# Hybrid attention block: the key and value projections as one unit of 512 columns, and the norm and rotation of the keys moved into the delta rule

## The chip, the cores and the metric

The kernel runs on one core of one Trainium2 chip. The metric is the device time of one execution in microseconds (us), as a median of several runs. The engines are TensorE (PE, with its weight loads as PEld), VectorE (DVE), ScalarE (ACT), GpSimd (POOL), and SyncE (SP), on whose queue all DMAs are issued. Each engine works through its instructions in order.

## What is computed

One layer of a decoder on x of 1024 tokens by 1024 channels, all in float32:

```python
h = rms_norm(x, norm_mix_g)
proj = h @ w_in
...
a_q = apply_partial_rope(rms_norm(a_q.reshape(B, S, ATT_HEADS, ATT_HEAD_DIM), q_norm_g), cos, sin)
a_k = apply_partial_rope(rms_norm(a_k.reshape(B, S, ATT_KV_HEADS, ATT_HEAD_DIM), k_norm_g), cos, sin)
a_v = a_v.reshape(B, S, ATT_KV_HEADS, ATT_HEAD_DIM)
...
o_att = dsa_sparse_attention(a_q, a_k, a_v, i_q, i_k, i_w)
merged = jax.nn.sigmoid(gate_a) * o_gdn + jax.nn.sigmoid(gate_b) * o_att
x = x + merged @ w_out
h2 = rms_norm(x, norm_mlp_g)
x = x + jnp.square(jax.nn.relu(h2 @ w_mlp_up)) @ w_mlp_down
```

proj is split into twelve parts, a_q (1024 columns), a_k (256) and a_v (256) among them. o_gdn is a gated delta rule over 8 heads (convolution, chunks of 64 tokens, a triangular solve, a scan of the state). The sparse attention scores every key for each query with a small indexer (i_q, i_k, i_w), takes the 256 best keys and attends to these alone.

## The kernel before

**Precision.** Each float32 operand of a projection is split into a high and a low part (hi, lo), and a product is three matmuls: hi by hi, hi by lo, lo by hi. ACT makes the high part of a weight (w<-wraw or w<-w), DVE the low part as the difference. The normed, transposed input stays in SBUF as ht_hi and ht_lo (hh and hl in the profile).

**Order of the work.** First the norm and transposition of x. Then the projections of the indexer and of the attention, in units: misc (unit 0), iq0 and iq1 (units 1 and 2, the indexer's queries), aq0 and aq1 (units 3 and 4, 512 columns each, called WIDE), ak (unit 5) and av (unit 6), 256 columns each. Beside them run the indexer's scores (sq<-ikh,iqt on PE, irl on ACT, sc on DVE) and the search for the 256th best score (tkcm passes on ACT, tkeq passes on DVE). Then come the eight heads of the delta rule, for which 48 units of 48 matmuls (gdense, dd<-hh,w) are put between as filler, then the attention, the output projection and the MLP.

**A unit.** The 1024 tokens are 8 blocks of 128, in two halves. For each block, dense and wide_dense add 8 tiles of 128 channels by three matmuls each, 24 matmuls, in one PSUM bank (name dd, two buffers), and ACT drains the bank to SBUF (drain, into tiles named pj and iq). A block of the units ak and av is 256 columns wide, so two blocks share a bank. In a WIDE unit the weights come in four pairs p of channel tiles; wide_weights casts the pair p of the next unit once the event ("pd", u - 1, p) says that the last matmul that uses it is issued. The ak and av weights are loaded and cast by weights, in two halves.

**After a unit.** proj_post takes four blocks of queries (or all eight of the keys): squares with row sums on ACT (hj), an inverse root in small steps on DVE (hss, hr, hrt), the product with it on DVE (pj<-pj,hr), the product with the gain on POOL (pj<-pj,qng, for the keys pj<-pj,kng), the rotation on POOL (ras, pj<-pj,ropeA), and a store to DRAM (QD, KD). The values (av) are stored as they come (VD).

**What sets the order.** All instructions are issued through Weave, a list scheduler that runs when the kernel is built: chains of work with priorities wait for events, each instruction has a modelled duration, and the result is one fixed order for each engine. It models no wait for a PSUM bank; such waits come from the tile framework, which makes a writer of a tile wait for the tile's earlier readers, whatever part of it they touch. The projections have priority 9, so they fill what the other chains leave. As all instructions pass one helper, they have one line in the profile (L2399), and are told apart by the names of their tiles.

**The end of the projections.** gweights loads and splits the weights of gdense; its first two units wait for the last projections' weights to be used, since they take the same slots. The scheduler runs until ak and av are stored, the tiles of this phase are given back, and the delta rule's chains are added. keys(h) is one of them; for every third head its tile um lies in slot 3.

Of the kernel before, what the change touches and what calls it, by code (L numbers as in the profile page):

```python
# [50 lines left out]
def body(tc, a, out, dbg=None):  # L51
# [51 lines left out]
    def rsq_w(pl, dst, src, n, tag, apart=True):  # L103
        t = pl.tile([P, max(n, 4)], F32, name=tag + "t")[:, :n]
        V_.tensor_scalar(dst.bitcast(I32), src.bitcast(I32), -0.5, float(0x5F3759DF), op0=OP.mult, op1=OP.add)
        for _ in range(3):
# [6 lines left out]
            if apart:  # L113
# [5 lines left out]
             + [("aq0", [(0, C_AQ, HALF)]), ("aq1", [(0, C_AQ + HALF, HALF)]), ("ak", [(0, C_AK, 256)]), ("av", [(0, C_AV, 256)])])  # L119
    WIDE = range(3, 5)  # L120
# [25 lines left out]
    kng = ix.tile([P, P], F32, name="kng")  # L146
# [18 lines left out]
    def loads():  # L165
# [31 lines left out]
        SY_.dma_start(kng, a["k_norm_g"].to_broadcast([P, P]))  # L197
# [131 lines left out]
    def weights(us):  # L329
        for u in us:  # L330
            yield
            if u == 5:
                yield ("pw", 4, 3)
            if u > 1:
                if u != 5:
                    yield ("pdense", u - 2)
# [11 lines left out]
            for js in ((0, 1),) if u == 1 else [(j,) for j in range(KT // kn)]:  # L348
                if u == 5:
                    yield ("pd", 4, js[0])  # L350
                yield "A"
                for j in js:
                    A_.activation(sp[j][0], sp[j][2], AF.Copy)
                if u == 1:
                    wv.done("w1hi")
                yield
                for j in js:
                    hi, lo, src = sp[j]
                    eng, nm = (G_, "G") if 0 else (V_, "V")
                    if u != 1:  # L360
                        yield nm
                    eng.tensor_tensor(lo, src, hi.bitcast(F32), op=OP.subtract)
                    hk += [hi[:, k, :] for k in range(kn)]
                    lk += [lo[:, k, :] for k in range(kn)]
                    if u in (1, 5):
# [3 lines left out]
            if u in (1, 5):  # L369
                load(u + 1)  # L370
# [10 lines left out]
    def wide_weights():  # L381
# [9 lines left out]
        for u in WIDE:  # L391
            for p in range(4):
# [11 lines left out]
                if u + 1 in WIDE:  # L404
                    wide_load(u + 1, p)
                elif p == 1:
                    load(u + 1)

    def wide_dense():
        for u in WIDE:  # L410
            for tb in range(NB):
                half, o = tb // 4, (tb % 4) * P
                if o == 0:
                    if u == 4:
                        yield ("stored", 3, 0) if half else ("score", 0)
                    outs[u, half] = ix.tile([P, 4, HALF], F32, name="iq" if u == 4 and half == 0 else "pj", bufs=2)
                    wv.add(3, proj_post(("pout", u, 4 * half + 3), (u, half), "aq", outs[u, half], 4 * half, 4, 4))
                ps = pd.tile([P, HALF], F32, name="dd")
                n = 0
                for k in range(KT):  # L420
                    if tb == 0 and k % 2 == 0:
                        yield ("pw", u, k // 2)
                    hi, lo = (t[:, k % 2, :] for t in whl[u, k // 2])
                    h_, l_ = ht_hi[k][half][:, o:o + P], ht_lo[k][half][:, o:o + P]
                    for l, r in ((h_, hi), (h_, lo), (l_, hi)):
                        PE_.matmul(ps, l, r, start=n == 0, stop=n == 3 * KT - 1)
                        n += 1
                        yield 0.0
                    if tb == NB - 1 and k % 2:
                        wv.done("pd", u, k // 2)  # L430
                wv.add(1, drain(outs[u, half][:, tb % 4, :], ps, ("pout", u, tb)))
            wv.done("pdense", u)

    def dense():
        jobs = [(0, 0), (1, 0), (0, 1), (1, 1), (1, 2)]
        jobs += [(2, t) for t in range(3)] + [(3, 0)] + [(u, t) for u in (5, 6) for t in range(4)]
        for u, t2 in jobs:
# [3 lines left out]
            nm = units[u][0]  # L441
# [11 lines left out]
            yield ("pwj", u, 0) if u in (1, 5) and t2 == 0 else ("pw", u)  # L453
# [15 lines left out]
            if t2 == 0:  # L469
                if nm[0] == "i":  # L470
                    outs[u] = ix.tile([P, 6, 256], F32, name="iq", bufs=2)
                    wv.add(1, iq_post(u - 1, outs[u]))
                else:
                    yield ("stored", 3, 1) if u == 5 else ("score", 1)
                    outs[u] = ix.tile([P, NB, 256], F32, name="pj" if u == 5 else "iq", bufs=2)
                    wv.add(3, proj_post(("pout", u, 3), (u,), nm, outs[u], 0, NB, 2))
# [3 lines left out]
            for j, ks in ((0, (0, 4)), (1, (0, 4)), (0, (4, KT)), (1, (4, KT))) if one else ((0, (0, KT)), (1, (0, KT))):  # L480
                tb = (2 if nm[0] == "i" else 0) + 2 * t2 + j
                half, o = tb // 4, (tb % 4) * P
                n = 3 * ks[0]
                for k in range(*ks):
                    if u == 1:
                        yield ("ht", half, k)
                        yield ("pwj", u, k // 4)
                    if u == 5 and t2 == 0:
                        yield ("pwj", u, k // 4)
# [188 lines left out]
    def proj_post(ready, key, nm, t, b0, nb, nh):  # L678
        yield ready
        dst = {"ak": KD, "av": VD, "aq": QD}[nm].rearrange("(b p) c -> p b c", p=P)[:, b0:b0 + nb, :]  # L680
        if nm == "aq":
            c0 = (key[0] - 3) * HALF
            dst = dst[:, :, c0:c0 + HALF]
        if nm != "av":
            gain = kng if nm == "ak" else qng
            v = t.rearrange("p b (h d) -> p b h d", h=nh)
            g = t.rearrange("p b (h d) -> p (b h) d", h=nh)
            ss = ix.tile([P, nb, nh], F32, name="hss", bufs=2)
            for b in range(nb):
                yield "A"  # L690
                for hh in range(nh):
                    junk = ix.tile([P, P], BF16, name="hj")
                    A_.activation(junk, v[:, b, hh, :], AF.Square, accum_out=ss[:, b, hh:hh + 1])
            yield
            sf = ss.rearrange("p b h -> p (b h)")
            V_.tensor_scalar(sf, sf, 1.0 / P, EPS, op0=OP.mult, op1=OP.add)
            yield
            r = ix.tile([P, nb, nh], F32, name="hr", bufs=2)
            rf = r.rearrange("p b h -> p (b h)")
            yield from rsq_w(ix, rf, sf, 16, "hr")  # L700
            yield
            V_.tensor_tensor(g, g, rf[:, :, None].to_broadcast([P, 16, P]), op=OP.mult)
            yield
            G_.tensor_tensor(g, g, gain[:, None, :].to_broadcast([P, 16, P]), op=OP.mult)
            yield from rope(ix, v, ropeA, nb, b0, nh, 16, "ra", G_)
# [4 lines left out]
        wv.done("stored", *key)  # L710

# [122 lines left out]
    wv.add(1, weights(range(5, len(units))))  # L834
# [157 lines left out]
    def keys(h):  # L992
# [3 lines left out]
        if h > 1:  # L996
            yield ("join", h - 2)
        es = gp.tile([P, NB, P], F32, name="es", bufs=3)
# [324 lines left out]
    for u in (6, 5):  # L1323
        wv.run(until=("put", u))
# [1040 lines left out]

class Ring:
# [102 lines left out]
```

## Time and profile before

| what | value |
|---|---|
| median of 3 runs | 1791.11 us (1791.09 to 1791.8) |
| span of the profiled execution | 1790.2 us |
| PE busy | 1775.3 us, 99% |
| DVE, ACT, POOL busy | 72%, 57%, 31% |
| granted TensorE clock | 1.00 in all stretches shown |

The profile has one execution, for which the page gives the span alone; it is 0.9 us below the median of the runs. A row of a timeline gives the start, the length, the engine, the tile written and the tiles read, the shape, how many such instructions in a row, and in brackets the idle time before it with what ended it. Since a matmul's end overlaps the next one's start, the rate is read from start to start.

### The profile page before, as it was taken

To read this page: it belongs to the slowest core of one execution; us is meant where nothing else is said; L and a number is where in the kernel's file an instruction comes from. 1 tells how busy PE (TensorE), PEld (TensorE's weight loads), DVE (VectorE), ACT (ScalarE), POOL (GpSimd) and SP (SyncE) were. 2 spreads that over 40 slices of the span, in tenths; PEclk is the share of its full clock that TensorE was granted. 3 is DMA by queue.
4 is the path that set the end of the run, shared out by engine and by line. 5 is a ranking of instruction groups with operands and counts; after the bars stand their busy time and mean duration, and the time that the engine had idled before them with its cause. 6 is when DMAs were issued, how large, how long until landed. Compare 5 with 4: busy or idle time off the path is not lost. (4 is left out here: it accounts for less than half of the span.)

```text
span 1790.2 us, 27615 instructions
## 1 busy us (share of the span) xinstructions
PE 1775.3 (99%) x9841; PEld 1486.8 (83%) x9841; DVE 1285.6 (72%) x2758; ACT 1013.4 (57%) x2074; POOL 548.6 (31%) x772
## 2 busy tenths in 40 slices
PE   9999999999999999999999999999999999999999
PEld 7987898888888888888887888888888888888887
DVE  6547668867787887975368776887666668969673
ACT  7555757666666554453447666686666664333331
POOL 0005430843462424554013211232333222222230
PEclk9999999999999999999999999999999999999999
DMA  5201242232222222332356231225444459373241
GB/s 165 83 13 48 72 122 73 50 99 66 69 75 72 54 66 56 89 85 54 101 179 205 71 102 54 94 94 183 153 161 145 143 192 372 122 249 127 95 139 49
DMA packets 196412, 198.73 MB, mean 111 GB/s; under 512 B 45146, under 2 KB 140595, under 8 KB 196275
## 3 DMA queue, kind: packets, MB, share of 16 engines
q1 hardware_dynamic: 196258, 196.98, 35.1%
q8 instruction: 77, 1.26, 0.3%
q14 instruction: 61, 0.49, 0.1%
q10 hardware_dynamic: 16, 0.00, 0.0%
HBM read 141.17 MB, written 55.77 MB: 110 GB/s over the span
## 5 line engine op out<-in xcount | busy, mean ns | idle before, releaser
L2399 PE MATMUL dd<-hh,w 128*128 128x512 f32 x1552 | 513.1, 402 | 0.0
L2399 PEld LDWEIGHTS dd<-hh,w 128*128 128x128 f32 x1552 | 285.6, 189 | 52.7 <-issue 2.1
L2399 PE MATMUL dd<-hl,w 128*128 128x512 f32 x776 | 312.3, 402 | 0.0
L2399 ACT ACTIVATE m<-m 128x512 fp32r<-128x512 f32 (+1 forms) x240 | 139.8, 625 | 79.4 <-PE o L2399 29.8
L2399 PE MATMUL dd<-hh,m 128*128 128x512 f32 x520 | 173.3, 397 | 0.1
L2399 DVE TENSOR_TENSOR m<-m,m 128x512 fp32r<-128x512 f32 (+2 forms) x184 | 141.0, 793 | 38.9 <-ACT m L2399 33.6
L2399 PEld LDWEIGHTS dd<-hl,w 128*128 128x128 f32 x776 | 146.4, 189 | 25.5 <-issue 0.4
L2399 PE MATMUL dd<-w,hh 128*128 128x256 f32 (+1 forms) x704 | 165.1, 324 | 0.0
L2399 PEld LDWEIGHTS dd<-w,hh 128*128 128x128 f32 x704 | 118.1, 190 | 9.7 <-issue 0.5
L2399 POOL TENSOR_TENSOR sx<-sx,stmp 128x60 f32<-128x60 f32 (+24 forms) x248 | 118.4, 477 | 19.4
L2399 POOL TENSOR_TENSOR stmp<-sx,um 128x60 f32<-128x60 f32 (+24 forms) x186 | 87.5, 470 | 91.7 <-DMA um<-ZA 78.1
L2399 PE MATMUL dd<-w,hl 128*128 128x256 f32 (+1 forms) x352 | 114.3, 325 | 0.0
L2399 PEld LDWEIGHTS dd<-hh,m 128*128 128x128 f32 x520 | 96.6, 188 | 18.4 <-DVE w L2399 0.7
L2399 DVE TENSOR_SCALAR_CACHE_REDUCE tkeq<-sc,cand 128x384 f16<-128x384 f32 (+3 forms) x128 | 103.3, 807 | 1.2
L2399 PE MATMUL dd<-hl,m 128*128 128x512 f32 x260 | 102.6, 395 | 0.9 <-POOL hl L2399 0.9
L2399 POOL TENSOR_TENSOR m<-m,m 128x512 f32<-128x512 f32 x48 | 69.7, 1459 | 105.7 <-DVE m L2399 59.0
L2399 ACT ACTIVATE hh<-m 128x1024 fp32r<-128x1024 f32 x44 | 45.2, 1056 | 90.9 <-PE s L2399 42.0
L2399 ACT ACTIVATE ha<-m 128x1024 fp32r<-128x1024 f32 x44 | 45.3, 1056 | 86.0 <-PE o L2399 35.1
L2399 DVE TENSOR_TENSOR w<-w,w 128x1024 fp32r<-128x1024 f32 (+1 forms) x63 | 69.3, 1102 | 24.6 <-ACT w L2399 23.1
L2399 ACT ACTIVATE tkcm<-sc,cand 128x1024 f16<-128x1024 f32 (+1 forms) x64 | 69.8, 1091 | 24.2 <-DVE cand L2399 23.4
L2399 PE MATMUL o<-hh,m 128*128 128x512 f32 x248 | 79.7, 389 | 0.0
L2399 PEld LDWEIGHTS dd<-w,hl 128*128 128x128 f32 x352 | 67.0, 190 | 4.6
(433 smaller groups left out, 4381.5 us busy)
## 6 DMA issues: line engine op xcount, KB each, us to landing
HD<-m SPq DMA_DIRECT2D x112, 256.0 KB
m<-HD SPq DMA_DIRECT2D x56, 512.0 KB
w<-in_w_in_dram SPq DMA_DIRECT2D x48, 512.0 KB
m<-in_w_mlp_up_dram SPq DMA_DIRECT2D x33, 512.0 KB
m<-in_w_mlp_down_dram SPq DMA_DIRECT2D x16, 512.0 KB
w<-in_x_dram SPq DMA_DIRECT2D x10, 512.0 KB
wraw<-in_w_in_dram SPq DMA_DIRECT2D x4, 1024.0 KB
es<-GC SPq DMA_DIRECT2D x8, 512.0 KB
```

Source lines behind the costliest of these rows:

```text
L2399: ins = f(*args, **kw)
```

## The change

The units ak and av become one WIDE unit akv (unit 5) of 512 columns. Keys and values are stored raw by put_raw, half by half. The blocks 6 and 7 of every query unit are now computed in turn, six matmuls of one weight pair for one block and then for the other, and the four blocks of akv's second half likewise, in four banks that are the halves of two tiles named sq; ("pd", u, p) is given after the pair's last use there. The keys' norm, gain and rotation become keys_normed, a chain of priority 7 which starts with the delta rule: four chunks of two blocks, each loaded from KD, treated by the same steps (normed, the middle of the old proj_post) and stored back. Its tiles are carved out of slot 3 (Carve), so keys(2) waits for it. gweights waits for single weight pairs of akv. The core of the diff:

```diff
@@ -116,8 +116,8 @@
-             + [("aq0", [(0, C_AQ, HALF)]), ("aq1", [(0, C_AQ + HALF, HALF)]), ("ak", [(0, C_AK, 256)]), ("av", [(0, C_AV, 256)])])
-    WIDE = range(3, 5)
+             + [("aq0", [(0, C_AQ, HALF)]), ("aq1", [(0, C_AQ + HALF, HALF)]), ("akv", [(0, C_AK, HALF)])])
+    WIDE = range(3, 6)
...
     def wide_dense():
         for u in WIDE:
-            for tb in range(NB):
-                half, o = tb // 4, (tb % 4) * P
...
-                ps = pd.tile([P, HALF], F32, name="dd")
...
-                    for l, r in ((h_, hi), (h_, lo), (l_, hi)):
-                        PE_.matmul(ps, l, r, start=n == 0, stop=n == 3 * KT - 1)
...
-                wv.add(1, drain(outs[u, half][:, tb % 4, :], ps, ("pout", u, tb)))
+            for half in range(2):
+                if u > 3:
+                    yield (("score", 0), ("stored", 3, 0), ("stored", 3, 1), ("score", 1))[2 * (u - 4) + half]
+                outs[u, half] = ix.tile([P, 4, HALF], F32, name="iq" if (u, half) in ((4, 0), (5, 1)) else "pj", bufs=2)
+                wv.add(3, (proj_post if u < 5 else put_raw)(("pout", u, 4 * half + 3), (u, half), "aq", outs[u, half], 4 * half, 4, 4))
+                if u == 5 and half:
+                    bank = [t[:, c, :] for t in (ps_.tile([P, 2, HALF], F32, name="sq") for _ in range(2)) for c in range(2)]
+                    order = [(range(4), (p, p + 1)) for p in range(4)]
+                else:
+                    bank = {}
+                    order = [((i,), (0, 4)) for i in range(4 - 2 * half)] + [((2, 3), (p, p + 1)) for p in range(4) if half]
+                for tbs, ks in order:
+                    for i in tbs:
+                        if ks[0] == 0 and not (u == 5 and half):
+                            bank[i] = pd.tile([P, HALF], F32, name="dd")
...
+                            for k in (2 * p, 2 * p + 1):
...
+                                for n, (l, r) in enumerate(((h_, hi), (h_, lo), (l_, hi))):
+                                    PE_.matmul(bank[i], l, r, start=k == n == 0, stop=k == KT - 1 and n == 2)
...
+                            if half and i == 3:
+                                wv.done("pd", u, p)
+                        if ks[1] == 4:
+                            wv.add(1, drain(outs[u, half][:, i, :], bank[i], ("pout", u, 4 * half + i)))
             wv.done("pdense", u)
+
+    def put_raw(ready, key, nm, t, b0, nb, nh):
+        for i in range(nb):
+            yield ("pout", 5, b0 + i)
+        for dst, o in ((KD, 0), (VD, 256)):
+            SY_.dma_start(dst.rearrange("(b p) c -> p b c", p=P)[:, b0:b0 + nb, :], t[:, :, o:o + 256])
+        wv.done("put", *key)
...
+    def keys_normed():
+        for b0 in range(0, NB, 2):
+            pl = Carve(slot(3, [P, D], F32))
+            t, table, gain = (pl.tile(d, F32) for d in ([P, 2, 256], [P, 2, 2, 32], [P, P]))
+            kd = KD.rearrange("(b p) c -> p b c", p=P)[:, b0:b0 + 2, :]
+            SY_.dma_start(t, kd)
+            SY_.dma_start(table, a["c_ropea"][:, :, b0:b0 + 2, :])
+            SY_.dma_start(gain, a["k_norm_g"].to_broadcast([P, P]))
+            yield
+            yield from normed(pl, t, 2, 2, 0, table, gain)
+            yield
+            SY_.dma_start(kd, t)
+            yield
+        wv.done("knorm")
...
     def gweights():
-        yield ("pdense", len(units) - 2)
+        for p in range(2):
+            yield ("pd", len(units) - 1, p)
         gload(0)
         for u in range(len(gunits)):
             yield
             if u == 1:
-                yield ("pdense", len(units) - 1)
+                yield ("pd", len(units) - 1, 2)
...
         if h > 1:
             yield ("join", h - 2)
+        if h == 2:
+            yield ("knorm",)
...
-    for u in (6, 5):
-        wv.run(until=("put", u))
+    wv.run(until=("put", 5, 1))
+    wv.add(7, keys_normed())
```

PE in the second half of unit 3 (aq0). dd_1450 before is the bank of block 6; after, dd_1448 is that of block 6 and dd_1459 that of block 7. Before:

```order
L2399 MATMUL dd_1450<-w6_750,hh1_99 128x512
L2399 MATMUL dd_1450<-w2_749,hl1_100 128x512
L2399 MATMUL dd_1450<-w3_793,hh2_101 128x512
L2399 MATMUL dd_1450<-w7_794,hh2_101 128x512
L2399 MATMUL dd_1450<-w3_793,hl2_102 128x512
```

After:

```order
L2435 MATMUL dd_1448<-w2_747,hh1_99 128x512
L2435 MATMUL dd_1448<-w6_748,hh1_99 128x512
L2435 MATMUL dd_1448<-w2_747,hl1_100 128x512
L2435 MATMUL dd_1459<-w2_747,hh0_97 128x512 [waits Activation_49]
L2435 MATMUL dd_1459<-w6_748,hh0_97 128x512
L2435 MATMUL dd_1459<-w2_747,hl0_98 128x512
```

Block 7, which stood 24 matmuls behind block 6's first, starts after six, and its first matmul waits for ACT (the drain of block 5, which used that bank).

ACT at the same place: irl is the indexer's relu, pj<-dd the drain, iqs and iqt belong to the next indexer block, w to the weights of unit 4. Before:

```order
L2399 ACTIVATE irl<-sq 128x512 [waits DVE_49,PE_49] x4
L2399 ACTIVATE pj<-dd 128x512
L2399 ACTIVATE iqs<-iq 128x8x64
L2399 ACTIVATE iqt<-tp 128x512 [waits PE_49]
L2399 ACTIVATE pj<-dd 128x512 [waits PE_49]
```

After:

```order
L2435 ACTIVATE irl<-sq 128x512 [waits DVE_49,PE_49] x4
L2435 ACTIVATE pj<-dd 128x512
L2435 ACTIVATE w_1469<-wraw 128x1024 [waits DMAHW3_49,PE_49]
L2435 ACTIVATE iqs<-iq 128x8x64
L2435 ACTIVATE w_1489<-wraw 128x1024 [waits DMAHW4_49,PE_49]
L2435 ACTIVATE iqt<-tp 128x512 [waits PE_49]
```

Two casts of unit 4's weights have moved ahead of the transposed indexer tile (iqt), one of them ahead of iqs; the drain still stands behind four irl.

PE at the end of akv. sq_2307 holds blocks 4 and 5, and the rows are the last matmul of block 4's last six and the first five of block 5's. After:

```order
L2435 MATMUL sq_2307<-w1_2119,hl7_112 128x512
L2435 MATMUL sq_2307<-w1_2119,hh6_109 128x512
L2435 MATMUL sq_2307<-w5_2120,hh6_109 128x512
L2435 MATMUL sq_2307<-w1_2119,hl6_110 128x512 [waits Activation_49]
L2435 MATMUL sq_2307<-w1_2119,hh7_111 128x512
L2435 MATMUL sq_2307<-w5_2120,hh7_111 128x512
```

The third of them waits for ACT, for the drain of block 4, which reads the same tile. At the end of av before, PE goes over to gdense, in dd banks:

```order
L2399 MATMUL dd_2655<-w5_2211,hh7_111 128x256
L2399 MATMUL dd_2655<-w1_2210,hl7_112 128x256
L2399 MATMUL dd_2727<-hh0_97,w6_2483 128x512 [waits Activation_49]
L2399 MATMUL dd_2727<-hl0_98,w6_2483 128x512
L2399 MATMUL dd_2727<-hh0_97,w7_2484 128x512 [waits DVE_49]
```

In both programs the first matmuls of gdense wait for the cast and the split of their weights; the waits inside the block are new. They come again in the second sq tile, between blocks 6 and 7.

More of the change, by code (lines that the diff above doesn't have):

```diff
@@ L432, in wide_dense @@
-            wv.done("pdense", u)
+            for half in range(2):
[13 more added lines that the diff above has]
+                            bank[i] = pd.tile([P, HALF], F32, name="dd")
+                        o = i * P
+                        for p in range(*ks):
+                            if half == 0 and i == 0:
+                                yield ("pw", u, p)
+                            for k in (2 * p, 2 * p + 1):
+                                hi, lo = (t[:, k % 2, :] for t in whl[u, p])
+                                h_, l_ = ht_hi[k][half][:, o:o + P], ht_lo[k][half][:, o:o + P]
+                                for n, (l, r) in enumerate(((h_, hi), (h_, lo), (l_, hi))):
+                                    PE_.matmul(bank[i], l, r, start=k == n == 0, stop=k == KT - 1 and n == 2)
+                                    yield 0.0
+                            if half and i == 3:
+                                wv.done("pd", u, p)
+                        if ks[1] == 4:
+                            wv.add(1, drain(outs[u, half][:, i, :], bank[i], ("pout", u, 4 * half + i)))
@@ L440, in dense @@
                 continue
-            nm = units[u][0]
             if u == 0 and t2 == 0:
@@ L452, in dense @@
                 continue
-            yield ("pwj", u, 0) if u in (1, 5) and t2 == 0 else ("pw", u)
+            yield ("pwj", u, 0) if u == 1 and t2 == 0 else ("pw", u)
             hi, lo = whl[u]
@@ L469, in dense @@
             if t2 == 0:
[L470 to L476, printed above, removed]
+                outs[u] = ix.tile([P, 6, 256], F32, name="iq", bufs=2)
+                wv.add(1, iq_post(u - 1, outs[u]))
             ps = pd.tile([P, 2, 256], F32, name="dd")
@@ L679, in proj_post @@
         yield ready
[L680 to L705, printed above, removed]
+        c0 = (key[0] - 3) * HALF
+        dst = QD.rearrange("(b p) c -> p b c", p=P)[:, b0:b0 + nb, c0:c0 + HALF]
+        yield from normed(ix, t, nb, nh, b0, ropeA, qng)
         yield
@@ L833, in body @@
     wv.add(1, wide_weights())
-    wv.add(1, weights(range(5, len(units))))
     wv.add(9, dense())
@@ L2362, in run, with __init__, tile @@
                 best[4] = y
+class Carve:
+    def __init__(self, tile):
+        self.t, self.n, self.named = tile, 0, {}
+    def tile(self, shape, dt, name=None, bufs=1):
+        if name in self.named:
+            return self.named[name]
+        n = math.prod(shape[1:])
+        w = n * (2 if dt == BF16 else 4) // 4
+        t = self.t[:, self.n:self.n + w]
+        self.n += w
+        t = t if dt == F32 else t.bitcast(dt)
+        names = "abc"[:len(shape) - 1]
+        if len(names) > 1:
+            t = t.rearrange(f"p ({' '.join(names)}) -> p {' '.join(names)}", **dict(zip(names[1:], shape[2:])))
+        if name is not None:
+            self.named[name] = t
+        return t
 class Ring:
```

58 lines of the change are left out of this document (27 added, 31 removed).

## The prediction

> **What bounds the kernel now.** I read the page's busy times first, then a table of stretches, then what TensorE (PE) waits for. The first row is the page's.
>
> ```profile
> PE 1775.3 (99%) x9841; PEld 1486.8 (83%) x9841; DVE 1285.6 (72%) x2758; ACT 1013.4 (57%) x2074; POOL 548.6 (31%) x772
> ```
>
> PE is idle for 1790.2 - 1775.3 = 14.9 us in all. The next rows are the stretches that the change can reach (from:to, length, busy time of PE, PEld, DVE, ACT, POOL, granted clock, DMA share, GB/s).
>
> ```profile
> 126.00:160.00 34.00, 31.55 (x147) 24.80 (x147) 21.45 (x26) 20.51 (x52) 16.54 (x20) 1.00 0.19 62
> 172.00:200.00 28.00, 27.67 (x124) 22.63 (x123) 20.43 (x46) 18.61 (x51) 13.04 (x20) 1.00 0.11 39
> 217.94:250.94 33.00, 33.00 (x278) 33.00 (x276) 22.54 (x65) 16.62 (x50) 18.48 (x25) 1.00 0.22 65
> 250.94:940.00 689.06, 689.06 (x4398) 573.77 (x4397) 511.94 (x1388) 384.01 (x895) 265.23 (x554) 1.00 0.30 82
> 940.00:990.00 50.00, 48.60 (x262) 39.34 (x260) 39.86 (x98) 37.55 (x76) 18.96 (x14) 1.00 0.59 185
> ```
>
> The projections of queries, keys and values lie in 126 to 251 us, the eight heads of the delta rule with their own projections in 251 to 940, and the attention begins about there. PE has no idle time at all from 250.94 to 940. The orders of before and after first differ at about 126 us of this trace and are the same again from about 990, so only these stretches can change. Their idle time is 34.00 - 31.55 = 2.45, then 28.00 - 27.67 = 0.33, then 50.00 - 48.60 = 1.40 us: 4.2 us. In the list of PE's waits for 126 to 990 us (total, times, longest) this is named:
>
> ```profile
> PE tp L2399 <- DVE iqs L2399: 1.3, 1, 1.3
> PE dd L2399 <- POOL hl L2399: 0.9, 1, 0.9
> PE sq L2399 <- ACT iqt L2399: 0.8, 1, 0.8
> PE sq L2399 <- ACT irl L2399: 0.6, 2, 0.3
> ```
>
> So a change of the projections gains by shorter PE work or by these few waits, and loses by any new wait of PE, for there is nothing else on the path.
>
> **The change, part by part.**
>
> *Matmuls.* The key and value units (ak, av) are 384 matmuls of 256 columns; the joined unit (akv) is 192 of 512. The first two rows group the PE matmuls of 126 to 252 us by shape; then come the weight loads of 217.94 to 250.94 (inside ak and av) and of 158.35 to 163.13 (512 columns).
>
> ```profile
> L2399 PE MATMUL dd<-w,hh 128*128 128x256 f32 x256 | 46.1, 283 | 0.0
> L2399 PE MATMUL dd<-w,hl 128*128 128x256 f32 x128 | 36.3, 283 | 0.0
> ```
>
> ```profile
> L2399 PEld LDWEIGHTS dd<-w,hh 128*128 128x128 f32 x184 | 28.7, 192 | 0.0
> L2399 PEld LDWEIGHTS dd<-w,hl 128*128 128x128 f32 x92 | 17.7, 192 | 0.0
> ```
>
> ```profile
> L2399 PEld LDWEIGHTS dd<-w,hh 128*128 128x128 f32 x14 | 2.6, 188 | 0.6
> L2399 PEld LDWEIGHTS dd<-w,hl 128*128 128x128 f32 x7 | 1.3, 188 | 0.3
> ```
>
> At 256 columns there is one load per matmul and PEld is never idle: 33.00 us / 276 = 0.1196 us from start to start. At 512 columns it is 4.78 us / 21 = 0.2276 and PEld has gaps. So 384 x 0.1196 = 45.9 us become 192 x 0.2276 = 43.7 us: **-2.2 us**, all on the path. The Trainium skill's page "TensorE: Matmul & The Clock Gate", section "Wait — 56ns, not 53.3ns?", speaks against most of it: it gives start to start as columns / 2.4 GHz plus about 2.5 ns once warm, so by the page halving the count would save 192 x 2.5 ns, an estimate of 0.5 us, and the sum below would be 1.7 us later. The rows differ from the page: they imply 2 x 0.1196 - 0.2276 = 0.0116 us a pair, over four times as much.
>
> *Two waits in akv's second half.* Its four blocks are computed in turn by weight pair, six matmuls each, in the halves of two tiles named sq. The order shows that the third matmul of the second block's last six waits for ACT's drain of the first block, in the same tile; so again in the other tile. That drain waits for the matmul issued just ahead, as it too sees one tile. The rows show a drain behind PE's last matmul, and PE behind an ACT result.
>
> ```profile
> 250.94 0.28 PE L2399 MATMUL dd<-w,hl 128*128 128x256 f32 x1
> ```
>
> ```profile
> 251.26 0.60 ACT L2399 ACTIVATE iq<-dd 128x512 f32<-128x512 f32 x1 [1.52 <-PE dd L2399]
> ```
>
> ```profile
> 150.64 0.60 ACT L2399 ACTIVATE iqt<-tp 128x512 fp32r<-128x512 f32 x1
> ```
>
> ```profile
> 151.29 0.50 PE L2399 MATMUL sq<-ikh,iqt 128*128 128x512 f32 x1 [0.78 <-ACT iqt L2399]
> ```
>
> ACT starts 251.26 - 251.22 = 0.04 us after a matmul's end, the drain lasts 0.60, PE starts 151.29 - 151.24 = 0.05 later. A matmul of 512 columns lasts 0.40 (the row at 251.06 below), and the next would have started 0.23 after its start. Each wait is 0.40 + 0.04 + 0.60 + 0.05 - 0.23 = 0.86 us: **+1.7 us** for both. Nothing covers it: PE is in order and its next work stands behind. Bounds: it can't be less than this if ACT is idle then, and +3.8 if each time one of ACT's search passes (1.15 us, a row below) has just begun.
>
> *Blocks 6 and 7 of the query units in turn.* In unit 3 block 7 starts six matmuls after block 6 and not 24, so it needs block 5's bank six matmuls into block 6. The rows, PE, DVE, ACT, POOL:
>
> ```profile
> 131.59 0.63 PE L2399 MATMUL dd<-w,hh 128*128 128x512 f32 x2
> ...
> 138.32 0.66 PE L2399 MATMUL tp<-identr,iqs 128*128 128x128 f32 x4 [1.33 <-DVE iqs L2399]
> ```
>
> ```profile
> 130.30 2.29 DVE L2399 TENSOR_TENSOR pj<-pj,hr 128x2048 f32<-128x2048 f32 x1
> 132.51 0.75 DVE L2399 SCALAR_TENSOR_TENSOR sc<-irl,iw,sc 128x512 f32<-128x512 f32 x1
> 134.98 3.28 DVE L2399 TENSOR_TENSOR iqs<-iq,iqs 128x512 fp32r<-128x512 f32 x1 [1.73 <-ACT iqs L2399]
> ```
>
> ```profile
> 133.35 0.60 ACT L2399 ACTIVATE irl<-sq 128x512 f32<-128x512 f32 x1 [1.89 <-DVE sc L2399]
> 133.84 0.59 ACT L2399 ACTIVATE pj<-dd 128x512 f32<-128x512 f32 x1
> ```
>
> ```profile
> 132.82 4.90 POOL L2399 TENSOR_TENSOR pj<-pj,qng 128x2048 f32<-128x2048 f32 x1 [3.95 <-DVE pj L2399]
> ```
>
> Block 6 starts at 131.59, so PE needs that bank at 131.59 + 6 x 0.2276 = 132.96. Its drain ends at 134.43, since the irl ahead of it on ACT waits for DVE's sc, and that for the 2.29 us multiply: 134.43 + 0.05 - 132.96 = a new wait of 1.5 us. The old wait of 1.33 us for the transposes (tp) goes, as these now come 28 matmuls after 131.59, at 131.59 + 28 x 0.2276 + 1.5 = 139.5, and were ready at 138.32 (up to 1.07 later now, one cast of weights stands ahead of them on ACT). Net **+0.2**; bounds -1.3 (the drain comes in time) and +1.5 (both waits stay). The other waits of this unit and the next (0.8 for iqt, 0.6 for irl) are drawn anew with ACT's order; I find like ones (a drain behind a cast, a transposed tile behind a drain) and take them as even, **0**, between -1.4 and +1.4.
>
> *Start of akv.* Its four weight pairs are cast by ACT and split by DVE as unit 4 lets go of them, the last only at unit 4's end. The rows are ACT, DVE and POOL at the start of ak now.
>
> ```profile
> 201.11 1.07 ACT L2399 ACTIVATE w<-wraw 128x1024 fp32r<-128x1024 f32 x1 [0.76 <-PE dd L2399]
> ...
> 203.94 1.15 ACT L2399 ACTIVATE tkcm<-sc,cand 128x1024 f16<-128x1024 f32 x1 [0.41 <-DVE cand L2399]
> ```
>
> ```profile
> 202.21 1.38 DVE L2399 TENSOR_TENSOR w<-wraw,w 128x1024 fp32r<-128x1024 f32 x1 [4.20 <-ACT w L2399]
> ```
>
> ```profile
> 197.90 4.60 POOL L2399 TENSOR_TENSOR iq<-iq,qng 128x2048 f32<-128x2048 f32 x1 [5.56 <-DVE tki L2399]
> ```
>
> The last pair is ready 1.07 + 1.38 = 2.5 us after unit 4's end, and PE asks for it after 18 matmuls, 18 x 0.2276 = 4.1 us: a cover of 1.6 us. One pass of the search on ACT (1.15) fits in it, two (2.3) don't: **+0.7**, between 0 and +1.9 (three).
>
> *Keys in the delta rule.* What unit ak did at its end, for all eight blocks, is now done in four chunks. DVE's first and last step now, beside POOL's multiply above (4.60 for the same shape) and one of its rotation steps (min/median/max in ns):
>
> ```profile
> 237.96 0.17 DVE L2399 TENSOR_SCALAR hss<-hss 128x16 f32<-128x16 f32 x1 [0.56 <-ACT hj L2399]
> ...
> 240.31 2.29 DVE L2399 TENSOR_TENSOR pj<-pj,hr 128x2048 f32<-128x2048 f32 x1
> ```
>
> ```profile
> L2399 POOL TENSOR_TENSOR pj<-pj,ropeA x14: 454/464/1388, 139.2 to 250.9; 128x128 f32<-128x128 f32 x12, 128x256 f32<-128x256 f32 x2
> ```
>
> A chunk costs DVE 240.31 - 237.96 = 2.35 of small steps, as many as before, and 2.29 / 4 = 0.57: 2.9 us; POOL 4.60 / 4 = 1.15 and eight rotation steps on a half or a quarter of that row's elements, at most 8 x 0.46: 4.8 us. What must be in time beside it is the next weights of the heads' projections:
>
> ```profile
> 251.06 0.40 PE L2399 MATMUL dd<-hh,w 128*128 128x512 f32 x1
> ```
>
> ```profile
> 251.75 1.05 ACT L2399 ACTIVATE w<-w 128x1024 fp32r<-128x1024 f32 x1
> ```
>
> ```profile
> 252.84 1.23 DVE L2399 TENSOR_TENSOR w<-w,w 128x1024 fp32r<-128x1024 f32 x1 [2.03 <-ACT w L2399]
> ```
>
> The weights split by 254.07 are used 48 matmuls after 251.06, at 262.0: a cover of 7.9 us, more than a chunk's 2.9 on DVE. On SP's queue each chunk puts three loads and a store, the store waiting for POOL; one weight load stands behind it, and those are issued more than a unit (10.9 us) ahead of use. I take **0**; it can't gain, as PE has no idle time there, and its other end is the slower case below. The end of the stretch, 940 to 990, is drawn anew: **0**, between -1.4 and +1.4.
>
> Sum: -2.2 + 1.7 + 0.2 + 0 + 0.7 + 0 + 0 = +0.4 us. The profiled execution's span is 1790.2, 0.9 below the median of the runs shown, 1791.1; with the same 0.9 the forecast is 1790.2 + 0.4 + 0.9 = **1791.5 us**. A measurement of this kernel can tell 0.2%, 3.6 us, from no change.
>
> **The rivals.**
>
> 1. *The saving stays and the waits go* (0.14). ACT's drains come in time, so the idle 2.8 us of 126 to 200 goes, and the 1.4 of 940 to 990 too: -2.2 + 1.7 - 2.8 - 1.4 = -4.7, 1786.4 us. For it: weights are released earlier by the new order of blocks 6 and 7. Against: the drain at 133.84, whose cause, DVE's 2.29 us, is untouched. If the 1.4 stays, it is 1787.8, within 0.2%.
> 2. *The new waits are hidden* (0.14). ACT drains a half before PE asks, or PE sees two halves as apart: -2.2 + 0.2 + 0.7 = -1.3, 1789.8 us. Against it are the waits written in the order.
> 3. *Slower: the chunks hold back the weights' low halves* (0.22). DVE's iqs above took 3.28 us inside POOL's multiply (132.82 to 137.72), where the six of this kind have these times (min/median/max in ns):
>
> ```profile
> L2399 DVE TENSOR_TENSOR iqs<-iq,iqs x6: 682/692/3281, 61.1 to 162.7; 128x512 fp32r<-128x512 f32 x6
> ```
>
> So a split that meets a chunk's POOL steps may last 4.8 and not 1.23 us, 3.6 more, and with the chunk's own 2.9 comes 6.5 us late. That is inside the cover of 7.9; it decides once 1.4 us of other DVE work are late too, which is not far, as DVE is busy for 44.5 of the 50 us from 300:
>
> ```profile
> 300.00:350.00 50.00, 50.00 (x250) 41.48 (x249) 44.50 (x111) 34.92 (x64) 32.66 (x61) 1.00 0.28 69
> ```
>
> With no cover left one chunk costs up to 6.5 us: 1791.5 + 6.5 = 1798.0. The Trainium skill, "GPSIMD Engine Reference", section "Specifications", says that POOL shares its SBUF interfaces with VectorE, in contention with DVE instructions of two inputs; the row agrees.
> 4. *The pitch follows the columns* (0.02), so that halving the count saves nothing: +2.6, 1793.7 us. The two pitches speak against it.
>
> **How the numbers follow.** The forecast's case has 0.48, with 1789.5 to 1794.5 as its own range. Rivals 2 and 4 are within 0.2% as well: same 0.48 + 0.14 + 0.02 = 0.64; faster 0.14; slower 0.22. The range reaches from 1787.0, where rival 1 without the last 0.6 us of its gain lies, to 1796.0, where two long bank waits (+2.1), the late last pair (+1.2) and one late split (+1.2) would put it.
>
> **What would show it.** Right: no 256-column matmul after unit 2's; 192 of pitch 0.2276 from about 205 us; two waits of PE on sq for ACT's iq of 0.86 us each near the end of akv; one wait of about 1.5 us for ACT's pj near 133 us, none for iqs near 139; no wait from akv's end to 940. It is wrong if PE waits in the delta rule for DVE's w, if akv's waits are absent or over 2 us each, or if the time leaves 1787.0 to 1796.0.

## The result and the profile after

| | before | after |
|---|---|---|
| median (lowest to highest), 4 runs each | 1791.45 us (1791.09 to 1792.24) | 1807.06 us (1804.62 to 1807.99) |
| ratio, 95% interval | | 1.0084, 1.0069 to 1.0098 |
| span of the profiled execution | 1790.2 us | 1806.1 us |

The change makes the kernel 15.6 us slower, outside the range on record. The page's busy times come first.

```profile
PE 1780.9 (99%) x9649; PEld 1478.0 (82%) x9649; DVE 1295.1 (72%) x2794; ACT 1013.7 (56%) x2074; POOL 563.4 (31%) x799
```

PE has 9841 - 9649 = 192 matmuls fewer, as it should. Its idle time is 1806.1 - 1780.9 = 25.2 us, where it was 14.9. The stretches after, with the columns of the prediction's table (the third ends where akv does, at 252.90):

```profile
126.00:160.00 34.00, 32.65 (x154) 26.55 (x154) 19.45 (x32) 21.64 (x57) 16.88 (x20) 1.00 0.30 93
172.00:200.00 28.00, 27.02 (x120) 21.76 (x119) 21.91 (x46) 19.82 (x52) 12.47 (x20) 1.00 0.11 39
204.60:252.90 48.30, 44.53 (x192) 35.54 (x192) 27.46 (x84) 21.97 (x58) 18.95 (x34) 1.00 0.27 88
252.90:930.00 677.10, 676.33 (x4315) 560.49 (x4314) 506.48 (x1372) 376.49 (x895) 280.59 (x583) 1.00 0.30 79
930.00:1010.00 80.00, 72.31 (x366) 57.24 (x365) 59.77 (x171) 52.42 (x112) 25.06 (x18) 0.96 0.58 185
```

The same last stretch of the kernel before:

```profile
930.00:1010.00 80.00, 78.52 (x408) 64.22 (x407) 63.70 (x179) 56.42 (x106) 24.83 (x19) 1.00 0.50 156
```

The loss isn't in the projections, where the change was made, and not in the delta rule, where the keys went (PE is idle for 0.8 of 677 us). It shows where the attention begins: 7.7 us idle in place of 1.5, and the granted clock falls to 0.96. Three rows of each trace say how the end of the delta rule stands to it (shortest, median, longest in ns, then first to last start): the last head's output (oo), the first of the attention's scores (s<-kTh), and the filler from the delta rule's own projections (dd<-hh,w). Before:

```profile
L2399 PE MATMUL oo<-svn,es x128: 270/275/276, 381.4 to 898.5; 128*128 128x128 f32 x128
L2399 PE MATMUL s<-kTh,qh x96: 274/389/501, 915.1 to 1133.3; 128*128 128x512 f32 x48, 128*128 128x256 f32 x32, 128*128 128x384 f32 x16
L2399 PE MATMUL dd<-hh,w x1536: 386/393/505, 251.1 to 940.5; 128*128 128x512 f32 x192
```

After:

```profile
L2435 PE MATMUL oo<-svn,es x128: 270/275/275, 384.1 to 913.2; 128*128 128x128 f32 x128
L2435 PE MATMUL s<-kTh,qh x96: 277/389/632, 930.4 to 1149.4; 128*128 128x512 f32 x48, 128*128 128x256 f32 x32, 128*128 128x384 f32 x16
L2435 PE MATMUL dd<-hh,w x1536: 387/392/506, 252.9 to 934.1; 128*128 128x512 f32 x192
```

The first filler starts 1.8 us later than before, the last head's last output 14.7 us later, the first score 15.3. The filler, though, ends 6.4 us earlier. Before, filler lay beside the attention for 940.5 - 915.1 = 25.4 us, now for 3.7. Counted in PE's order, of the 2304 filler matmuls (48 units of 48, dd<-hh,w and dd<-hl,w) 60 stood behind the first score before, and 9 do now. From the first filler to the first score PE does 4264 matmuls before and 4315 after; counted by tile, the 51 more are filler, and nothing else differs. PE's timeline after shows what follows (start, length, tile written and tiles read, how many, idle time before with its releaser):

```profile
933.90 0.40 PE L2435 MATMUL dd<-hl,w 128*128 128x512 f32 x1
934.13 0.39 PE L2435 MATMUL dd<-hh,w 128*128 128x512 f32 x1
935.22 0.38 PE L2435 MATMUL s<-kTh,qh 128*128 128x256 f32 x1 [0.70 <-ACT qh L2435]
935.45 0.28 PE L2435 MATMUL s<-kTl,qh 128*128 128x256 f32 x1
936.87 0.39 PE L2435 MATMUL s<-kTh,qlo 128*128 128x256 f32 x1 [1.14 <-DVE qlo L2435]
...
939.96 0.78 PE L2435 MATMUL o<-ph,vh 128*128 128x512 f32 x1
940.54 0.63 PE L2435 MATMUL o<-pl,vh 128*128 128x512 f32 x1
```

From the first row to the second it is 0.23 us. The last filler is at 934.13, and after it PE waits at one step of the attention after the other. At 940 a matmul of 512 columns takes 0.58 from start to start. Windows on this place:

```profile
935.00:945.00 10.00, 7.87 (x36) 6.27 (x36) 8.75 (x29) 5.82 (x18) 2.34 (x2) 0.83 0.79 283
945.00:950.00 5.00, 4.59 (x19) 3.12 (x18) 4.80 (x16) 2.77 (x5) 1.29 (x1) 1.00 1.03 359
950.00:955.00 5.00, 2.76 (x13) 1.46 (x12) 3.14 (x12) 4.83 (x8) 1.51 (x1) 1.00 0.31 90
955.00:960.00 5.00, 5.00 (x21) 4.11 (x20) 3.70 (x9) 3.40 (x7) 2.51 (x2) 0.66 0.80 258
```

The clock falls twice, to 0.83 over 10 us and to 0.66 over 5 us. That costs 10 x 0.17 + 5 x 0.34 = 3.4 us.

**The loss in stages.** ACT's first drain of unit 3 (92.1 before, 92.6 after) stands at the start of the projections touched, the first filler matmul at their end, and the 151st o<-p matmul inside the attention. Start: +0.5. Projections: 160.30 - 158.96 = +1.3. First filler to the 151st o<-p: 858.13 - 843.88 = +14.3. The rest: 695.06 - 695.22 = -0.2. The sum, 15.9, is the difference of the spans. The forecast for the second was +0.4, for the third 0.

**The theories.** *Order*: the scheduler draws the order of the delta rule anew, since its start, its first waits and keys(2) have moved. In the new draw the last head ends later, and 60 - 9 = 51 filler matmuls have gone ahead of the first score. At 0.226 us each (the prediction's rate is 0.2276, and a row further down gives 0.2252) that is 11.5 us of filler that the start of the attention no longer has beside it; its chain of small steps takes about as long as before and leaves PE waiting. *Chunks*: the keys' new work on DVE, POOL and SP holds up the heads (rival 3, in another form). *Local*: the waits of the projections, drains and POOL's product, are what counts.

### The profile page after: what moved, and what is told of

It reads as the page before. It is cut to its first block, busy times and chain, and to the rows that moved or that the text cites. A ratio compares the mean times of both kernels' runs of the same rounds, so it can differ in the third digit from the quotient of the medians.

```text
span 1806.1 us, 27351 instructions
## 1 busy us (share of the span) xinstructions
PE 1780.9 (99%) x9649; PEld 1478.0 (82%) x9649; DVE 1295.1 (72%) x2794; ACT 1013.7 (56%) x2074; POOL 563.4 (31%) x799
## 4 chain that ended last, share of the span: by engine, by line
PE 90%; DVE 3%; ACT 3%; issue 2%; DMA 1%; POOL 1%; SPq 0%; POOLq 0%; ACTq 0%; DVEq 0%
PE dd L2435 51%; PE o L2435 15%; PE s L2435 7%; PE pt L2435 6%; PE tt L2435 3%; PE sq L2435 3%; PE cc L2435 2%; PE oo L2435 1%; PE jj L2435 1%; DVE sc L2435 1%; DVE w L2435 1%; ACT hj L2435 1%; ACT irl L2435 1%; DMA w<-in_w_out_dram 0%; POOL hl L2435 0%
## 5 line engine op out<-in xcount | busy, mean ns | idle before, releaser
L2435 PE MATMUL dd<-w,hh 128*128 128x512 f32 (+1 forms) x512 | 139.1, 354 | 4.3 <-ACT pj L2435 1.9
L2435 POOL TENSOR_TENSOR stmp<-sx,um 128x60 f32<-128x60 f32 (+24 forms) x186 | 91.9, 494 | 97.1 <-DMA um<-ZA 57.1
L2435 PEld LDWEIGHTS dd<-w,hh 128*128 128x128 f32 x512 | 89.6, 189 | 17.7 <-DVE w L2435 3.3
L2435 PE MATMUL dd<-w,hl 128*128 128x512 f32 (+1 forms) x256 | 90.4, 353 | 0.0
L2435 ACT ACTIVATE tkcm<-sc,cand 128x896 f16<-128x896 f32 (+1 forms) x64 | 70.0, 1094 | 24.6 <-DVE cand L2435 21.6
L2435 ACT ACTIVATE w<-w 128x1024 fp32r<-128x1024 f32 (+1 forms) x64 | 55.5, 869 | 39.8 <-PE dd L2435 37.9
```

The costliest lines, as they stand in the source:

```text
L2435: ins = f(*args, **kw)
```

## The experiments

The runs of the kernel before beside them have medians of 1792.2 to 1792.3 us. "Filler" is the number of filler matmuls behind the first score in PE's order, "first score" its start in the profiled execution, and "rest" the span less that start. "Projections" is from the first drain of unit 3 to the first filler, "then" from there to the 151st o<-p.

| run | median us | ratio, 95% interval | filler | first score | rest | projections | then |
|---|---|---|---|---|---|---|---|
| before | 1791.45 | | 60 | 915.1 | 875.1 | 158.96 | 843.88 |
| after | 1807.06 | 1.0069 to 1.0098 | 9 | 930.4 | 875.7 | 160.30 | 858.13 |
| e1_select_later | 1796.48 | 1.0014 to 1.0032 | 60 | 919.9 | 875.2 | 160.27 | 846.77 |
| e2_no_chunks | 1805.51 | 1.0058 to 1.0092 | 9 | 928.6 | 873.2 | 160.21 | 854.56 |
| e3_before_redrawn | 1801.11 | 1.0031 to 1.0061 | 27 | 923.8 | 875.8 | 158.91 | 852.01 |
| e4_pair_drains | 1793.16 | 0.9997 to 1.0016 | 60 | 915.7 | 875.5 | 158.34 | 846.07 |
| e5_pool_split | 1789.63 | 0.9978 to 0.9995 | 60 | 912.4 | 875.5 | 155.58 | 844.36 |
| e6_two_step | 1791.05 | 0.9985 to 1.0003 | 61 | 911.8 | 878.2 | 153.92 | 848.11 |
| e7_no_chunks_select | 1795.26 | 1.0011 to 1.0030 | 60 | 917.8 | 874.9 | 160.27 | 845.62 |
| e8_all_select3 | 1788.28 | 0.9968 to 0.9986 | 60 | 910.0 | 874.9 | 153.92 | 844.35 |
| e9_before_pool_split | 1804.92 | 1.0058 to 1.0089 | 9 | 926.5 | 874.5 | 156.64 | 857.61 |

The rest is about 875 us whatever the filler (e2 is 2 us under it, and e6 3 over). That is the loss in one column: a kernel that has done 51 filler matmuls more ahead of its first score should be 11.5 us shorter behind it, and is not. In after, the 3.4 us of the clock are in the rest, so 875.1 + 3.4 - 875.7 = 2.8 us of the 11.5 are won back there; in e2, whose clock stays at 1.00, it is 1.9. Ahead of the first score, 51 filler matmuls are not quite all: from the first filler on the stretch grows by 13.5 us, which is 11.5 of filler, 0.8 of PE's idle time and 1.2 that no row shown names.

### e1: another draw of the same change

The chain that selects the keys starts 1.0 us later by the scheduler's own clock. No instruction is added.

```diff
         yield ("search", 7)
+        yield 1.0
```

> The changed kernel, with one line: the chain that turns the scores into masks (select) starts 1.0 us later by the planner's own clock. No instruction is added and none waits longer on the chip; only the fixed orders are drawn anew. Theory (order): the loss comes from the plan of the last head, after which 9 filler matmuls of the heads' projections are left when the attention's scores begin, against 60 before the change; here 60 are left again, so the waits of PE near 934 to 1005 us go and what stays is the redrawn projections: 1792 to 1796 us. Rival (the moved work): the key chunks' work on DVE, POOL and SP holds up the heads; it is all still there, so 1803 to 1808 us.

Measured: 1796.48 us, 0.5 above the end of the order theory's range and far below the other. The whole change is in it, and two thirds of the loss are gone. Its last stretch, and the score and filler:

```profile
930.00:1010.00 80.00, 78.53 (x407) 64.06 (x406) 63.32 (x166) 56.10 (x109) 26.35 (x20) 1.00 0.51 166
```

```profile
L2436 PE MATMUL s<-kTh,qh x96: 274/389/500, 919.9 to 1138.2; 128*128 128x512 f32 x48, 128*128 128x256 f32 x32, 128*128 128x384 f32 x16
L2436 PE MATMUL dd<-hh,w x1536: 387/392/506, 253.0 to 945.3; 128*128 128x512 f32 x192
```

Filler lies beside the attention for 25.4 us again, PE is idle for 1.5 us, and the clock is 1.00. The projections are those of after (160.27), so they aren't what the 10.6 us between the two came from.

### e2: the change without the chunks

This kernel leaves out the norm, gain and rotation of the keys.

```diff
-    wv.add(7, keys_normed())
+    wv.done("knorm")
```

> The changed kernel without the key chunks: the keys stay raw (their norm, gain and rotation are left out), nothing of them runs in the delta rule. The order of the last head still leaves 9 filler matmuls at the attention's start. Theory (order): the attention's start is as late as in the changed kernel, 1801 to 1808 us. Rival (the moved work): without it the loss goes, 1790 to 1795 us.

Measured: 1805.51 us, 9 filler left. The chunks are not the cause. Its last stretch is idle like that of after, at a clock of 1.00 in the profiled execution:

```profile
930.00:1010.00 80.00, 72.33 (x375) 56.62 (x374) 62.56 (x178) 55.62 (x117) 26.37 (x19) 1.00 0.55 181
```

From the first filler on it takes 854.56 - 843.88 = 10.7 us more than before, about the 11.5 of 51 filler matmuls. In after it is 14.3, and 3.4 of that is the clock. The four runs of after agree: 1807.85 and 1807.99 us at a mean clock of 0.998, 1806.27 at 0.999, 1804.62 at 1.000.

### e3: a draw of the kernel before

Nothing of the change is in it; the chain that selects the keys has another priority.

```diff
-    wv.add(8, select())
+    wv.add(3, select())
```

> The kernel before, with one number: the priority of the chain select is 3 and not 8. The same instructions, in an order in which 27 filler matmuls of the heads' projections are left when the attention's scores begin, and not 60. Theory (order): slower than before with no change of the projections or the keys, 1795 to 1801 us, with new waits of PE between 925 and 1000 us. Rival (the moved work, or the projections): 1790.5 to 1792.5 us.

Measured: 1801.11 us, 0.1 above the end of the order theory's range and 8.8 above the kernel before in the same session, with 27 filler left. Its last stretch:

```profile
930.00:1010.00 80.00, 74.88 (x379) 60.40 (x378) 62.19 (x171) 53.84 (x107) 27.24 (x20) 0.96 0.52 170
```

The projections take 158.91 us as before (158.96), so the whole loss is in the order behind them. It lies between the other two cases in filler, and in time too. 33 filler matmuls are 7.5 us and the clock of 0.96 another 80 x 0.04 = 3.2, while the stage "then" grew by 8.1: here too 2.6 us are won back behind the first score.

### e4: the false waits of akv taken out

The four drains of akv's second half are issued two by two, when both halves of an sq tile are complete; a draw with 60 filler.

```diff
-                            wv.add(1, drain(outs[u, half][:, i, :], bank[i], ("pout", u, 4 * half + i)))
+                            for j in ((i - 1, i) if i % 2 else ()) if u == 5 and half else (i,):
+                                wv.add(1, drain(outs[u, half][:, j, :], bank[j], ("pout", u, 4 * half + j)))
...
         yield ("search", 7)
+        yield 0.5
```

> The changed kernel with ACT's drains of akv's second half issued two by two, after both blocks of a sq tile are done, so that no matmul waits inside a tile; select starts 0.5 us later by the planner's clock, which leaves 60 filler matmuls at the attention's start. Theory (order, and the two bank waits as predicted): as the first run less two waits of 0.85 us, 1790.5 to 1794.5 us, and no wait of PE on sq for ACT's iq. If the waits are hidden by something else, the same time as the first run.

Measured: 1793.16 us. PE has no wait on sq for ACT's iq any more, and the projections are 160.27 - 158.34 = 1.9 us shorter than in e1. The forecast had 1.7 for the two waits. So the whole change, with a draw that keeps the filler and without the two waits, is within 0.2% of the kernel before. What is left of PE's waits at 126 to 260 us (total, times, longest) are those for drains in units 3 and 4, two at the start of akv, and one for the indexer:

```profile
PE dd L2437 <- ACT pj L2437: 1.9, 2, 1.3
PE dd L2437 <- DVE cand L2437: 1.4, 1, 1.4
PE dd L2437 <- DVE w L2437: 1.0, 1, 1.0
PE sq L2437 <- ACT irl L2437: 0.5, 1, 0.5
```

### e5: POOL's product in pieces

At the start of akv, a small step of DVE stood still inside POOL's product with the gain. In the trace of after, DVE and POOL:

```profile
199.63 0.15 DVE L2435 TENSOR_SCALAR tki<-cnt 128x1 int32<-128x1 f32 x1
199.70 4.30 DVE L2435 TENSOR_SCALAR cand<-thr 128x4 int32<-128x4 int32 x1
```

```profile
198.45 5.52 POOL L2435 TENSOR_TENSOR iq<-iq,qng 128x2048 f32<-128x2048 f32 x1 [5.49 <-DVE cand L2435]
```

The step on four columns takes 4.30 us and ends 0.03 us after POOL's product does. The step on one column ahead of it took 0.15, inside the same product. e5 is e4 with that product in four pieces, and another step length in the model.

```diff
-        G_.tensor_tensor(g, g, gain[:, None, :].to_broadcast([P, n, P]), op=OP.mult)
+        for b in range(0, n, 4):
+            yield
+            G_.tensor_tensor(g[:, b:b + 4, :], g[:, b:b + 4, :], gain[:, None, :].to_broadcast([P, 4, P]), op=OP.mult)
...
-        yield 0.5
+        yield 1.0
```

> The fourth run's kernel with POOL's product with the gain cut into pieces of four heads (128x512), so that a query half has four short ones and not one of 4.6 to 5.5 us; select starts 1.0 us later by the planner's clock, which leaves 60 filler matmuls at the attention's start. Theory (POOL's long product shuts DVE out: a DVE step of 128x4 elements lasted 4.30 us beside it at 199.70 us, and the low halves of akv's weights came late): the waits of 0.7, 1.2 and 1.5 us at akv's start go or fall below 0.5 each, and the time is 1789.5 to 1792 us. Rival (ACT's and DVE's search passes are ahead of the casts): the waits stay and so does the time, 1792.5 to 1794.5 us.

Measured: 1789.63 us. In its trace the same DVE step, POOL's four pieces, and the one wait that stayed:

```profile
201.11 1.19 DVE L2439 TENSOR_SCALAR cand<-thr 128x4 int32<-128x4 int32 x1
```

```profile
196.59 6.94 POOL L2439 TENSOR_TENSOR iq<-iq,qng 128x512 f32<-128x512 f32 x4 [8.73 <-DVE tki L2439]
```

```profile
208.60 0.50 PE L2439 MATMUL dd<-w,hh 128*128 128x512 f32 x1 [1.21 <-DVE w L2439]
```

After had three waits at 194 to 212 us: 0.5 for ACT's drain at 194, 1.0 at 208 and 1.4 at 211. The last two are for the low halves of akv's third and fourth weight pair, which DVE splits (the view puts the second down to cand, but the split ends 0.06 us before PE starts). In after:

```profile
207.29 1.22 DVE L2435 TENSOR_TENSOR w<-misc,w 128x1024 fp32r<-128x1024 f32 x1
...
210.18 1.36 DVE L2435 TENSOR_TENSOR w<-wr,w 128x1024 fp32r<-128x1024 f32 x1 [0.16 <-ACT hj L2435]
```

In e5 the first two of the three waits are gone. The one that stayed is for the fourth pair:

```profile
205.85 1.01 DVE L2439 TENSOR_SCALAR_CACHE_REDUCE tkeq<-sc,cand 128x768 f16<-128x768 f32 x1
...
207.34 1.21 DVE L2439 TENSOR_TENSOR w<-wr,w 128x1024 fp32r<-128x1024 f32 x1
```

Its split ends at 208.55, 0.05 before PE's matmul. The step on DVE takes 1.19 us, and the projections are 158.34 - 155.58 = 2.8 us shorter, 1.2 of it the third pair's wait. The forecast of the time held, that of the waits held in part: POOL's product is the cause of the third pair's wait and not of the fourth's.

### e6: blocks 6 and 7 in turn by halves of the weights

```diff
-[((2, 3), (p, p + 1)) for p in range(4) if half]
+[((2, 3), ks) for ks in ((0, 2), (2, 3), (3, 4)) if half]
```

> The run above, with the blocks 6 and 7 of units 3 and 4 taking their first two weight pairs at once, twelve matmuls and not six, so that block 7 asks for its bank 1.37 us later; the order leaves 61 filler matmuls at the attention's start. Theory (the wait of 1.35 us at 134 us is that for block 5's drain): it falls to 0.2 us or less, and the first filler matmul starts 1.0 to 1.5 us earlier than in the run above. The time: 1788.5 to 1792.5 us, as the end of the delta rule is planned anew once more. Rival (another wait takes its place, that of the transposes for iqs): no gain at that stage.

Measured: 1791.05 us. The wait in unit 3 fell from 1.4 to 0.3 us, where 0.2 or less was expected, and the projections are 1.7 us shorter. The total isn't better: the order was drawn anew once more, and "then" takes 3.8 us more with 61 filler left, 0.9 of it ahead of the first score and 2.8 behind. Between 300 and 1010 us PE waits 1.7 us for POOL's hl and 1.1 for DVE's am. In e8, another draw with the same edits, "then" is 844.35, so the filler left isn't all that a draw sets.

### e7: e1 without the chunks

> The first run's kernel (select 1.0 us later) without the key chunks; the keys stay raw (their norm, gain and rotation are left out). 60 filler matmuls at the attention's start, as in the first run, so the two differ by the chunks alone. Theory (the chunks are hidden behind the filler): 1795.0 to 1797.0 us, within 1 us of the first run. Rival (the chunks cost what the second run was faster than the changed kernel, 1.6 to 3.5 us): 1792.5 to 1794.5 us.

The edits are those of e1 and e2 together. Measured: 1795.26 us, against 1796.48 with the chunks. This kernel leaves out the norm, gain and rotation of the keys as well. With the filler equal, the chunks cost about 1.2 us at most, after the first filler (846.77 - 845.62); the intervals of the two ratios overlap, so it isn't clear of the noise. The forecast's time held, its bound of 1 us did not quite.

### e8: all edits, and the priority of e3

e6 without its modelled step, and with select() at priority 3.

> The sixth run's kernel (drains two by two, POOL's product in pieces, twelve matmuls at once), with select not later but at priority 3, after which 60 filler matmuls are left at the attention's start. In the kernel before, priority 3 cost 8.8 us. Theory (order): the priority counts only for the order it happens to give, so here it is no loss: the sixth run's first filler matmul at about 246.5 us, with a tail as in the fifth run, 1787.5 to 1790 us. Rival (priority 3 slows the heads by itself): 1794 us or more.

Measured: 1788.28 us, ratio 0.9977 (0.9968 to 0.9986): 4.0 us less than the kernel before beside it. The priority that cost the kernel before 8.8 us costs nothing here; its first score is at 910.0 with 60 filler behind it. So it isn't the priority that is good or bad, but the draw.

### e9: the kernel before with POOL's product in pieces

```diff
-            G_.tensor_tensor(g, g, gain[:, None, :].to_broadcast([P, 16, P]), op=OP.mult)
+            for b in range(0, 16, 4):
+                yield
+                G_.tensor_tensor(g[:, b:b + 4, :], g[:, b:b + 4, :], gain[:, None, :].to_broadcast([P, 4, P]), op=OP.mult)
```

> The kernel before, with nothing of the change, and POOL's product with the gain cut into pieces of four heads. The order that the planner makes of it leaves 9 filler matmuls at the attention's start, as the changed kernel's does. Theory (order): the loss of the changed kernel without its change, 1801 to 1807 us, with PE's waits between 930 and 1005 us. Rival (the loss belongs to the projections or the keys): 1790 to 1793 us.

Measured: 1804.92 us. This has nothing of the change, is 158.96 - 156.64 = 2.3 us faster in the projections, and loses 12.6 us all the same:

```profile
L2401 PE MATMUL s<-kTh,qh x96: 277/389/562, 926.5 to 1144.3; 128*128 128x512 f32 x48, 128*128 128x256 f32 x32, 128*128 128x384 f32 x16
L2401 PE MATMUL dd<-hh,w x1536: 387/392/502, 248.3 to 930.2; 128*128 128x512 f32 x192
```

```profile
930.00:1010.00 80.00, 72.05 (x364) 56.71 (x363) 61.90 (x170) 53.75 (x112) 26.34 (x19) 0.98 0.53 174
```

Filler beside the attention for 3.7 us, 8 us idle: the profile of after again. So an edit that has nothing of the change can bring this draw.

## Why the prediction was wrong

**The step that failed** is the last one of the parts: "The end of the stretch, 940 to 990, is drawn anew: 0, between -1.4 and +1.4." That it is drawn anew was right. The bound was not: 1.4 us was the idle time that PE had there, so it bounds what a new draw can gain, and says nothing of what it can lose. The prediction let the attention begin at about 940. Its first score stood at 915.1, so the last 25 us of the stretch that it read as a delta rule without idle time were already the attention, and PE had no idle time in them because 60 filler matmuls lay beside its first steps. Had the prediction asked what covers those steps, as it did for the weights' low halves, the bound above would have been 60 x 0.226 = 13.6 us, near the 14.3 measured, of which 3.4 are the clock. The same step left the order of the heads out: it looked for waits in the delta rule, and there are next to none (0.8 us in all, and none of them for DVE's w; between 300 and 930 us the list has one row of 0.2 us). The lateness of the last head is in the order itself. That order could be read before the run, as the 60 and the 9 could.

**What held.**

- *Matmuls.* -2.2 was forecast, from 0.2276 us a matmul. A stretch inside akv without idle time has 25.00 / 111 loads = 0.2252:

```profile
215.00:240.00 25.00, 25.00 (x112) 20.71 (x111) 17.39 (x57) 10.23 (x23) 10.68 (x19) 1.00 0.39 128
```

  192 x 0.2252 = 43.2, against 45.9 before: -2.7. The Trainium skill, "TensorE: Matmul & The Clock Gate", section "Wait — 56ns, not 53.3ns?", by which the prediction estimated a saving of 0.5 us, differs from this row as well.
- *The two waits in akv's second half.* 0.86 each was forecast. PE and ACT at the first:

```profile
246.87 0.61 PE L2435 MATMUL sq<-w,hh 128*128 128x512 f32 x2
248.17 0.50 PE L2435 MATMUL sq<-w,hl 128*128 128x512 f32 x1 [0.69 <-ACT iq L2435]
```

```profile
247.52 0.60 ACT L2435 ACTIVATE iq<-sq 128x512 f32<-128x512 f32 x1 [4.68 <-PE sq L2435]
```

  The second matmul starts at 246.87 + 0.23 = 247.10, and the third 1.07 behind it in place of 0.23: 0.84 us lost, and again at 251.87. e4 shows that the drains of the shared tile are the cause, and rival 2 falls.
- *Blocks 6 and 7 in turn.* A wait of 1.5 us at 133 was forecast:

```profile
133.21 0.39 PE L2435 MATMUL dd<-w,hl 128*128 128x512 f32 x1
134.95 0.72 PE L2435 MATMUL dd<-w,hh 128*128 128x512 f32 x2 [1.35 <-ACT pj L2435]
```

  134.95 - 133.21 - 0.23 = 1.51 lost, and no wait for the transposes behind it. e6 shows that it falls to 0.3 when block 7 starts later. Rival 1 falls with it.

**What was mis-sized.** The start of akv was put at +0.7. Two matmuls wait there:

```profile
207.17 0.40 PE L2435 MATMUL dd<-w,hh 128*128 128x512 f32 x1
208.57 0.50 PE L2435 MATMUL dd<-w,hh 128*128 128x512 f32 x1 [1.01 <-DVE w L2435]
...
211.60 0.50 PE L2435 MATMUL dd<-w,hh 128*128 128x512 f32 x1 [1.39 <-DVE cand L2435]
```

The first lost 208.57 - 207.17 - 0.23 = 1.17 us, the second 1.55 by the same reckoning: +2.7, above the bound of 1.9. The prediction had counted search passes on ACT; what came late was DVE's split. For the third pair the cause is POOL's product, as e5 shows. The prediction had the row for that (3.28 us for iqs inside POOL's multiply) and used it for rival 3 alone. The fourth pair's wait stays with the product in pieces, so its cause is another. In e5's rows its split stands behind a search pass on DVE; that this pass is the cause wasn't tested. The terms then are -2.7 + 1.7 + 0.2 + 2.7 = +1.9, where +1.3 was measured; the remaining -0.6 is within the ±1.4 kept for the other waits of units 3 and 4, which went from 1.4 us (0.8 and 0.6) to 1.0 (0.5 for a drain, 0.5 for irl).

**The keys** were put at 0 in the delta rule. They cost about 1.2 us at most (e1 against e7). Rival 3 had the right sign at 0.22, but not the mechanism: PE doesn't wait for DVE's w in the heads, and without the chunks the loss stays (e2).

**What stays open.** Two things were not found: why the split of akv's fourth pair comes late (e5), and what makes up the 1.2 us ahead of the first score that no row shown names. Why a given edit yields one draw or the other wasn't settled; e3, e8 and e9 show only that it doesn't follow from the edit's kind. What akv alone would bring with an equal order is known for its own stage, not for the whole: 158.34 against 158.96 with the drains in pairs (e4), and 155.58 against 156.64 with POOL's product in pieces on both sides (e5 and e9), so 0.6 to 1.1 us less.

## What to carry to other kernels

Where one list scheduler draws the whole program, an edit is a change of its own stage plus a new draw of all that comes behind; judge the stage by its own length, and read the draw from the order before any run: where the last chain lands, and how much filler is left when the next stage starts. A stretch in which PE is never idle is covered by something; its bound on the slow side is about the size of that cover (here 13.6 us), not the idle time that is left. Before a change is dropped for a loss behind its stage, try another draw of it: here a model step of 1.0 us without any instruction was worth 10.6 us.

## What the runs showed of the hardware

- POOL's product of 128x2048 held up a DVE step until it ended: the step on 128x4 took 4.30 us, and 1.19 with the product in pieces. A step on 128x1 inside the same product took 0.15. The Trainium skill, "GPSIMD Engine Reference", section "Specifications", names a contention of POOL with DVE instructions that have two inputs in SBUF or run in a 2-port mode. The row of two inputs (3.28 us for iqs) agrees; the step on 128x4 has one input, and no row shows its mode.
- The granted clock fell without any long stop: to 0.83 in a stretch of 10 us with 2.1 us idle, and to 0.66 in the 5 us after one with 2.2 us idle, where no single wait of PE at 930 to 1010 us was over 1.2 us. It did so in some executions and not in others of the same program: the four runs of after go from 1804.62 us at a mean clock of 1.000 to 1807.99 at 0.998. Why it falls in one and not in another isn't shown.
